# One layer of a hybrid attention, convolution and MoE block: q/k stacks two tiles late, rotation ahead of the head norm, expert weights by half rows

## The chip, the cores and the metric

One Trainium2 chip, of which the program uses one core. The time of a run is the device time of that core in microseconds (us). The core has five engines that each work through an instruction list of their own, in order: TensorE (PE, matmuls and transposes; PEld is its weight load), VectorE (DVE), ScalarE (ACT), GpSimd (POOL) and SyncE (SP, which mostly issues DMAs). The order within each list is fixed when the program is built. PSUM is the memory that PE writes to, SBUF the memory of the other operands.

## The reference

```python
def in_proj(h, w_in, q_g, k_g):
    z = h @ w_in
    ...
    q = rms_norm(q.reshape(b, s, N_HEADS, HEAD_DIM), q_g)
    k = rms_norm(k.reshape(b, s, N_KV_HEADS, HEAD_DIM), k_g)
...
def apply_axial_rope(x, cos, sin):
    xs = x.reshape(*x.shape[:-1], 2, 2, ROPE_FREQS)
    x1, x2 = xs[..., 0, :], xs[..., 1, :]
    c, s = cos[:, None], sin[:, None]
    return jnp.stack([x1 * c - x2 * s, x1 * s + x2 * c], axis=-2).reshape(x.shape)
...
    hx = rms_norm(x, norm1_g) * (1.0 + sc1) + sh1
    hc = rms_norm(ctx, norm1_g) * (1.0 + csc1) + csh1
    qx, kx, vx, bx, cx, ux = in_proj(hx, w_in, q_norm_g, k_norm_g)
    qc, kc, vc, bc, cc, uc = in_proj(hc, w_in, q_norm_g, k_norm_g)
    qx = apply_axial_rope(qx, cos, sin)
    kx = apply_axial_rope(kx, cos, sin)
...
    ax = latent_attention(qx, k_all, v_all)
    convx = short_conv(bx, cx, ux, conv_w)
    x_new = x + gt1 * merge_out(ax, convx, attn_out_g, conv_out_g, w_out)
    hx2 = rms_norm(x_new, norm2_g) * (1.0 + sc2) + sh2
    x_new = x_new + gt2 * hier_moe(hx2, w_group, w_router, w_gate, w_up, w_down)
...
    def expert_block(args):
        xb, e = args
        return (jax.nn.silu(xb @ w_gate[e]) * (xb @ w_up[e])) @ w_down[e]
```

There are 2048 latent tokens and 256 context tokens of 1024 features, 8 query heads and 2 key/value heads of 64, 8 channel groups of the convolution, and 32 experts of width 768 with two experts for each token. Everything is float32 in the inputs and the output. The output is the final RMSNorm of x_new.

## The kernel before

Matmuls run in float16 on split operands: a float32 value is written as a high part (a cast) and a low part (the value minus the high part), and three matmuls (high by high, high by low, low by high) stand for one.

**Projection of q, k and v** (45 to 285 us). The tokens go by chunks of 256 (two tiles of 128): one of context, then eight of latent tokens. `norm_load` brings two tiles `xt` in and scales their rows (L184 on ACT, L186 on POOL). `norm_T` works for the next chunk: for each of 8 feature blocks k, PE transposes (L268), ACT applies the modulation into `hf` (L270), DVE makes the high part of `h` (L271) and the low part (L272), each 128x256. `project` computes for a tile 24 pairs of matmuls into `pq` (L303, 512 columns) and `pk` (L304, 256 columns), and after each block k calls the generator `beside`, which lets other work into PE's list between the matmuls. `head_norm` follows: squares on ACT (L314, L315), their sum `ssq` (L318, DVE), the reciprocal root `qnr` by a power on POOL (L117), the product with q and k out of PSUM into `z` (L321, L322), the rotation by `rope` out of SBUF (L288, L292, L293), the float16 stacks `ks` and `qs` (ACT L333, L339; DVE L334, L340). The rotation tables, norm gain included, are made for all ten heads on POOL (L283). `stacks` transposes `ks` and `qs` on PE (L347, L348, L357) and ACT copies them out (L349, L350, L358). Its steps are written into the last two blocks of the next tile's projection and the first two of the tile after that; the scheduler may place PE's instructions somewhat off those places. In PE's list the `ks` transposes of a chunk's first tile stand in the last block (k = 7) of the next tile's projection, those of its second tile in the second block (k = 1) of the tile after next.

**Attention, convolution, output projection and routing** (285 to 1565 us) aren't written differently by the change. `mod2` computes the second half of the modulation row by row on DVE there (`macc`, L655), from DMAs on SP.

**Experts** (1565 to 2624 us). `PLAN` is a fixed list that mixes large and small experts (room for 104 to 208 tokens). `Stream` brings each expert's weights in as six pieces of 1536 KB (`raw`, 5 buffers, DMAs on SP) and splits each in three steps (L1192 on ACT, L1194 on DVE, 128x1024 each) into `wr` (6 buffers). `gate_up` goes over 6 column blocks f: 24 matmuls for gate, 24 for up (L1338 to L1340), then silu (ACT L1356), product (DVE L1357), cast (ACT L1358) and low part (DVE L1359) into `a`; after each of the first five f come three split steps. `down` (more than 128 tokens, with `rows_out`, L1412 and L1413) or `down_rows` (L1396, L1399) holds four. Pieces are column halves: gate 1, up 1, gate 2, up 2, down 1, down 2, so that a row of a DMA is 384 or 512 numbers long. `transposes` (L1332 to L1334) makes the next expert's input. Results are added to `acc` in DRAM by POOL's indirect DMAs; at the end the final norm loads `acc` through the same `raw` buffers (`final_item`).

Of the kernel before, what the change touches and what calls it, by code (L numbers as in the profile page):

```python
# [19 lines left out]
P = 128  # L20
D = 1024
# [23 lines left out]
WS = 256.0  # L45
NRAW, NRDY, NEARLY = 5, 6, 4
# [12 lines left out]
def tile_block(ctx: ExitStack, tc: tile.TileContext, x, c, ctxt, c_ctx, w_mod, b_mod, norm1_g, w_in,  # L59
# [80 lines left out]
    with ExitStack() as st:  # L140
# [112 lines left out]
        g10 = wp.tile([P, 2, 10, HD], F32, name="g10")  # L253
        V.tensor_copy(g10[:, 0, 0:8], gqk[:, 0:1].to_broadcast([P, 8, HD]))
        V.tensor_copy(g10[:, 0, 8:10], gqk[:, 1:2].to_broadcast([P, 2, HD]))
        gs = [g10[:, i].rearrange("p h (a b f) -> p (h a) b f", a=2, b=2) for i in range(2)]
# [5 lines left out]
        def norm_T(xs, ch):  # L262
            i = 1 if ch < 0 else 0
            h = hcur[ch] = hp.tile([P, 2, KT, CH], F16, name="h")
            for k in range(KT):
                tp = pp.tile([P, CH], F32, name="tp", bufs=2)
                for j, xn in enumerate(xs):
                    T.transpose(tp[:, j * P:(j + 1) * P], xn[:, k * P:(k + 1) * P], ident)  # L268
                hf = sp.tile([P, CH], F32, name="hf")
                A.activation(hf, tp, AF.Identity, scale=AB[:, i, 0, k:k + 1], bias=AB[:, i, 1, k:k + 1])  # L270
                V.tensor_copy(h[:, 0, k, :], hf)  # L271
                V.tensor_sub(h[:, 1, k, :], hf, h[:, 0, k, :])  # L272
                if k == KT - 1 and ch >= 0:
                    nc.scalar.dma_start(hs[ch], h.rearrange("p a k t -> p (a k t)"))
                yield

        def rope_tables(tt):
            rt_ = qp.tile([P, 2, HD], F32, name="rt_")
            nc.sync.dma_start(rt_[:, 0], rope_c[tt * P:(tt + 1) * P, :])
            nc.sync.dma_start(rt_[:, 1], rope_s[tt * P:(tt + 1) * P, :])  # L280
            tab = qp.tile([P, 2, 10, HD], F32, name="tab")
            for i in range(2):
                G.tensor_tensor(tab[:, i], g10[:, i], rt_[:, i:i + 1].to_broadcast([P, 10, HD]), op=OP.mult)  # L283
            return tab

        def rope(dst, z, tab):
            t1 = qp.tile([P, 10, HD], F32, name="rp1", bufs=1)
            V.tensor_mul(t1, z, tab[:, 0])  # L288
            t2 = qp.tile([P, 10, HD], F32, name="rp2", bufs=1)
            zv, tv, sv = [t.rearrange("p h (a b f) -> p (h a) b f", a=2, b=2) for t in (z, t2, tab[:, 1])]  # L290
            for b in range(2):
                V.tensor_mul(tv[:, :, b], zv[:, :, 1 - b], sv[:, :, b])  # L292
            V.tensor_add(dst, t1, t2)  # L293
# [14 lines left out]
        def head_norm(pq, pk, tt, lat, tab):  # L308
            kt = tt + 2 if lat else tt
            nh = 10 if lat else 2  # L310
            z = qp.tile([P, 10, HD], F32, name="z")
# [4 lines left out]
            A.activation(vf[:, kt, :], pk[:, 128:256], AF.Copy, scale=1.0 / WS)  # L316
            ssq = qp.tile([P, 10], F32, name="ssq")
            V.tensor_reduce(ssq[:, 0:nh], sq[:, 0:nh], axis=AX.X, op=OP.add)  # L318
            r = rstd_of(qp, ssq[:, 0:nh], nh, 1.0 / (HD * WS * WS), "qn")
            if lat:  # L320
                V.tensor_mul(z[:, 0:8], pq.rearrange("p (h d) -> p h d", d=HD), r[:, 0:8, None].to_broadcast([P, 8, HD]))  # L321
            V.tensor_mul(z[:, nh - 2:nh], pk[:, 0:128].rearrange("p (h d) -> p h d", d=HD),  # L322
                         r[:, nh - 2:nh, None].to_broadcast([P, 2, HD]))
            V.tensor_reduce(vmx[:, kt:kt + 1], vf[:, kt, :], axis=AX.X, op=OP.max, apply_absolute_value=True)
            if lat:
                zr = qp.tile([P, 10, HD], F32, name="zr")
                rope(zr, z, tab)
            else:
                V.tensor_mul(z[:, 0:2], z[:, 0:2], gqk[:, 1:2].to_broadcast([P, 2, HD]))
                zr = z  # L330
# [41 lines left out]
        for ch in range(-1, NCH):  # L372
# [3 lines left out]
            for j in range(CH // P):  # L376
# [3 lines left out]
                def beside(first, second, j=j):  # L380
# [9 lines left out]
                z = project(h, j, lat, beside(done, nxt))  # L390
# [3 lines left out]
                if len(done) > 1:  # L394
                    for _ in done.pop(0):
                        pass
# [3 lines left out]
            if ch + 2 < NCH:  # L400
                xs = norm_load(ch + 2, (A, G))
# [729 lines left out]
    HE = DE // 2  # L1131
    PW = KT * HE

    def piece_src(e, i):
        if i < 4:
            src = (w_gate, w_up)[i % 2][0, bass.ds(e, 1)].rearrange("a (k p) n -> p (a k) n", p=P)
            return src[:, :, (i // 2) * HE:(i // 2 + 1) * HE], KT
        src = w_down[0, bass.ds(e, 1)].rearrange("a (k p) n -> p (a k) n", p=P)
        return src[:, :, (i - 4) * 512:(i - 3) * 512], FT

    class Stream:
# [62 lines left out]
        def get(self, q):  # L1204
            while self.piece <= q:
                assert self.step()
            return self.ready[q].rearrange("p a (k n) -> p a k n", k=KT if q % 6 < 4 else FT)
# [92 lines left out]
    with ExitStack() as st:  # L1300
# [16 lines left out]
        def gather(il):  # L1317
            xg = []
            for i, (t, o, n) in enumerate(il):
                g_ = xp.tile([P, D], F32, name=f"xg{i}", bufs=3 - i)  # L1320
# [15 lines left out]

        def three(p_, w, k, cs, x, C, first, last):
            T.matmul(p_[:, :C], w[:, 0, k, cs], x[:, 0, k, :C], start=first, stop=False)  # L1338
            T.matmul(p_[:, :C], w[:, 0, k, cs], x[:, 1, k, :C], start=False, stop=False)  # L1339
            T.matmul(p_[:, :C], w[:, 1, k, cs], x[:, 0, k, :C], start=False, stop=last)  # L1340
# [266 lines left out]
```

## Time and profile before

| | us |
|---|---|
| median of 3 runs | 2630.31 (2628.85 to 2637.18) |
| profiled execution | 2625.82 |
| its span | 2624.0 |
| PE busy | 2333.0 (89%) |
| DVE busy | 2064.2 (79%) |
| ACT busy | 1678.6 (64%) |
| POOL busy | 726.3 (28%) |
| mean granted clock of PE | 0.95 of full speed |

The span is the time from the first to the last instruction that the profile holds; the 1.8 us that the execution takes beyond it lie around it. An engine is busy while it works on an instruction; matmuls overlap in PE's pipeline, so that the durations of single matmuls add up to more than PE's busy time. A wait is put down to the instruction that ended it. The granted clock says how fast PE was allowed to run: 1.0 is 2.4 GHz and 0.5 is 1.2 GHz, and means lie between. The chain of waits is followed back from the last instruction, at each step to what released it.

### The profile page before, as it was taken

How to read it: one execution, taken by the hardware profiler on the slowest of the kernel's cores; microseconds unless marked ns; L12 is line 12 of the kernel's file. 1: busy time of each engine (PE TensorE's matmuls, PEld its weight loads, DVE VectorE, ACT ScalarE, POOL GpSimd, SP SyncE). 2: the span in 40 equal slices, each digit the busy share in tenths (PEclk: the TensorE clock that was granted, in tenths of full speed). 3: DMA queues.
4: the chain of work that ended last, by engine and by line, in shares of the span. 5: the costliest groups of instructions: out<-in, count | busy, mean ns of one | idle time of the engine just before them, and what ended most of it. 6: DMA issues, size and time to landing. Idle time of an engine off the chain costs nothing. (4 is left out here: it accounts for less than half of the span.)

```text
span 2624.0 us, 65043 instructions
## 1 busy us (share of the span) xinstructions
PE 2333.0 (89%) x26923; PEld 1791.5 (68%) x26923; DVE 2064.2 (79%) x3558; ACT 1678.6 (64%) x3170; POOL 726.3 (28%) x449
## 2 busy tenths in 40 slices
PE   7878898898999999888889949999999999999974
PEld 2545565665777755555555539998899988999953
DVE  4786789999777788878897657788788887788866
ACT  4554365566666676556656427777677777888854
POOL 2554114322222234435444331111111111211122
PEclk9888999999999999889998969999999999999987
DMA  7422423323111143212211569999999999999996
GB/s 279 145 90 88 127 78 115 125 82 108 50 52 34 34 93 81 64 52 80 58 64 52 191 197 336 338 326 304 307 355 350 349 334 344 340 335 340 358 311 247
DMA packets 320331, 499.27 MB, mean 190 GB/s; under 512 B 50466, under 2 KB 229022, under 8 KB 316959
## 3 DMA queue, kind: packets, MB, share of 16 engines
q1 hardware_dynamic: 281142, 429.41, 48.7%
q0 software_dynamic: 16032, 39.85, 6.0%
q10 hardware_dynamic: 22856, 25.82, 2.9%
q8 instruction: 212, 3.47, 0.5%
q14 instruction: 89, 0.72, 0.1%
HBM read 427.20 MB, written 67.90 MB: 189 GB/s over the span
## 5 line engine op out<-in xcount | busy, mean ns | idle before, releaser
L1194 DVE SCALAR_TENSOR_TENSOR wr<-raw,wr 128x1024 f16<-128x1024 f32 x576 | 685.4, 1218 | 118.8 <-ACT wr L1192 111.3
L1192 ACT ACTIVATE wr<-raw 128x1024 f16<-128x1024 f32 x576 | 580.4, 1054 | 57.3 <-DMA raw<-in_w_up_dram 22.9
L489 ACT ACTIVATE pf<-st 128x512 f32<-128x512 f32 x576 | 345.0, 599 | 284.2 <-PE st L488 226.9
L496 POOL TENSOR_TENSOR pl<-pf,ph 128x1024 f16<-128x1024 f32 x125 | 273.5, 2188 | 620.0 <-PE o L514 259.3
L461 DVE TENSOR_REDUCE mx<-mxp 128x1 f32<-128x512 f32 (+1 forms) x640 | 391.9, 628 | 65.1 <-PE mxp L460 63.6
L1339 PEld LDWEIGHTS <-wr 128*128 128x128 f16 x4032 | 397.4, 99 | 27.6 <-issue 24.6
L1340 PEld LDWEIGHTS <-wr 128*128 128x128 f16 x4032 | 397.2, 99 | 14.4 <-issue 9.9
L1338 PEld LDWEIGHTS <-wr 128*128 128x128 f16 x4032 | 397.1, 99 | 14.1 <-issue 11.3
L490 ACT ACTIVATE ph<-st 128x512 f16<-128x512 f32 x576 | 344.6, 598 | 0.0
L1338 PE MATMUL pg<-x,wr 128*128 128x152 f16 (+19 forms) x1536 | 293.9, 226 | 6.7 <-ACT sg L1356 3.8
L1338 PE MATMUL pu<-x,wr 128*128 128x152 f16 (+19 forms) x1536 | 293.7, 226 | 5.2 <-DVE sg L1357 5.1
L1340 PE MATMUL pu<-x,wr 128*128 128x152 f16 (+19 forms) x1536 | 293.1, 226 | 1.6 <-DVE wr L1194 0.8
L1340 PE MATMUL pg<-x,wr 128*128 128x152 f16 (+19 forms) x1536 | 293.5, 226 | 1.1 <-DVE wr L1194 1.0
L1339 PE MATMUL pg<-x,wr 128*128 128x152 f16 (+19 forms) x1536 | 293.8, 226 | 0.0
L1339 PE MATMUL pu<-x,wr 128*128 128x152 f16 (+19 forms) x1536 | 293.5, 226 | 0.0
L613 PE MATMUL z<-h,cwh 128*128 128x256 f16 x1536 | 275.1, 275 | 12.9 <-DVE vb L621 8.9
L460 PE MATMUL mxp<-k1T,q 128*128 128x512 f16 (+1 forms) x640 | 230.9, 364 | 41.5 <-DVE mx L461 40.5
L514 PE MATMUL o<-vh,pl 128*128 128x65 f16 x2304 | 246.2, 196 | 7.0 <-DVE pl L498 4.6
L512 PE MATMUL o<-vh,ph 128*128 128x65 f16 x2304 | 247.0, 197 | 0.3 <-ACT ob L521 0.2
L513 PE MATMUL o<-vlo,ph 128*128 128x64 f16 x2304 | 246.8, 195 | 0.0
L512 PEld LDWEIGHTS <-ph 128*128 128x128 f16 x2304 | 217.6, 99 | 25.2 <-issue 9.8
L487 PE MATMUL st<-q,k1T 128*128 128x512 f16 x576 | 222.5, 387 | 12.4 <-ACT ph L490 11.9
(349 smaller groups left out, 5541.6 us busy)
## 6 DMA issues: line engine op xcount, KB each, us to landing
raw<-in_w_down_dram SPq DMA_DIRECT2D x64, 1536.0 KB
raw<-in_w_gate_dram SPq DMA_DIRECT2D x63, 1536.0 KB
raw<-in_w_up_dram SPq DMA_DIRECT2D x63, 1536.0 KB
xt<-in_x_dram SPq DMA_DIRECT2D x32, 512.0 KB
h<-hs SPq DMA_DIRECT2D x16, 1024.0 KB
wmod<-in_w_mod_dram SPq DMA_DIRECT2D x64, 256.0 KB
w<-in_w_mod_dram SPq DMA_DIRECT2D x16, 512.0 KB
hs<-h ACTq DMA_DIRECT2D x8, 1024.0 KB
```

What stands on the lines that cost most here:

```text
L461: V.tensor_reduce(rowmax[u][:, j, i:i + 1], p_[:, :n], axis=AX.X, op=OP.max)
L489: A.activation(pf[:, i], p_, AF.Exp)
L490: A.activation(ph[:, i], p_, AF.Exp)
L496: G.tensor_tensor(pl, pf, ph, op=OP.subtract)
L512: T.matmul(po[:, j], ph[:, i, js], vh1[:, k, g], start=f, stop=False, skip_group_check=True)
L513: T.matmul(po[:, j, 0:HD], ph[:, i, js], vlo[:, k, g], start=False, stop=False, skip_group_check=True)
L613: T.matmul(z, w_[:, k, cs], h[:, a_, k, :], start=(n == 0), stop=(n == 3 * KT - 1))
L1192: A.activation(w[:, 0, sl], t[:, sl], AF.Copy, scale=WS)
L1194: V.scalar_tensor_tensor(w[:, 1, sl], t[:, sl], WS, w[:, 0, sl], op0=OP.mult, op1=OP.subtract)
L1338: T.matmul(p_[:, :C], w[:, 0, k, cs], x[:, 0, k, :C], start=first, stop=False)
L1339: T.matmul(p_[:, :C], w[:, 0, k, cs], x[:, 1, k, :C], start=False, stop=False)
L1340: T.matmul(p_[:, :C], w[:, 1, k, cs], x[:, 0, k, :C], start=False, stop=last)
```

## The change

It has five parts.

1. `beside` steps one generator, the stacks of the tile two back, at the odd blocks k of the projection.
2. `head_norm` rotates q and k straight out of PSUM (`pq`, `pk`), adds, and only then multiplies by the head norm (one product over all ten heads, L334 of the change). The tables `tab` hold one row for q and one for k.
3. `norm_T` makes the high and the low part of `h` for four feature blocks at once (`HB`, 128x1024), and moves on at the even blocks k, and at all blocks of a chunk's second tile.
4. The second `xt` of a chunk is scaled on ACT.
5. Expert pieces are halves by rows (gate 1, gate 2, up 1, up 2, down 1, down 2), so that a DMA's row is 768 or 1024 numbers long. `gate_up` does the six gate blocks, then the six up blocks, with one split step after each; `down` and `down_rows` use both halves from their start and hold six steps.

```diff
+HB = 4
...
-        g10 = wp.tile([P, 2, 10, HD], F32, name="g10")
...
+        gx = wp.tile([P, 2, HD], F32, name="gx")
...
         def norm_T(xs, ch):
...
+            for b in range(KT // HB):
+                hf = sp.tile([P, HB, CH], F32, name="hf")
+                for k2 in range(HB // 2):
+                    tp = pp.tile([P, 2, CH], F32, name="tp", bufs=2)
...
+                    if k2 == HB // 2 - 1:
+                        ks = slice(b * HB, (b + 1) * HB)
+                        V.tensor_copy(h[:, 0, ks], hf)
+                        V.tensor_sub(h[:, 1, ks], hf, h[:, 0, ks])
...
-                G.tensor_tensor(tab[:, i], g10[:, i], rt_[:, i:i + 1].to_broadcast([P, 10, HD]), op=OP.mult)
+            for i, g_ in enumerate((gqk, gx)):
+                G.tensor_tensor(tab[:, i], g_, rt_[:, i:i + 1].to_broadcast([P, 2, HD]), op=OP.mult)
...
+        def rope(zr, pq, pk, tab):
...
+            for o, n, src, i in ((0, 8, pq, 0), (8, 2, pk[:, 0:2 * HD], 1)):
+                zv = src.rearrange("p (h d) -> p h d", d=HD)
+                V.tensor_tensor(t1[:, o:o + n], zv, tab[:, 0, i:i + 1].to_broadcast([P, n, HD]), op=OP.mult)
...
+                for b in range(2):
+                    V.tensor_tensor(ts[:, :, :, b], zs[:, :, :, 1 - b], ss_[:, :, :, b].to_broadcast([P, n, 2, 16]), op=OP.mult)
+            V.tensor_add(zr, t1, t2)
...
-                V.tensor_mul(z[:, 0:8], pq.rearrange("p (h d) -> p h d", d=HD), r[:, 0:8, None].to_broadcast([P, 8, HD]))
...
+            V.tensor_mul(zr[:, 0:nh], zr[:, 0:nh], r[:, 0:nh, None].to_broadcast([P, nh, HD]))
...
+                def beside(behind, second, j=j):
                     for k in range(KT):
-                        if k < 2 and len(first) > 1:
-                            next(first[0], None)
-                        if k >= KT - 2 and first:
-                            next(first[-1], None)
-                        if k % 2 or (j and k == KT - 2):
+                        if k % 2 and behind:
+                            next(behind, None)
+                        if k % 2 == 0 or j:
                             next(second, None)
                         yield
...
+                behind = done.pop(0) if len(done) > 1 else None
+                z = project(h, j, lat, beside(behind, nxt))
...
-                xs = norm_load(ch + 2, (A, G))
+                xs = norm_load(ch + 2, (A, A))
...
+    KN = (KT // 2, KT // 2, FT // 2)
+    PW = KT // 2 * DE
...
+        kn = KN[i // 2]
+        src = (w_gate, w_up, w_down)[i // 2][0, bass.ds(e, 1)].rearrange("a (k p) n -> p (a k) n", p=P)
+        return src[:, (i % 2) * kn:(i % 2 + 1) * kn, :], kn
...
+        def both(self, q):
+            return self.get(q), self.get(q + 1)
...
+            sg = sp.tile([P, FT, CM], F32, name="sg", bufs=1)
+            for m in range(2):
+                w = ws.both(q0 + 2 * m)
+                for f in range(FT):
+                    p_ = pp.tile([P, 512], F32, name=("pg", "pu")[f % 2])
+                    for k in range(KT):
+                        three(p_, w, k, slice(f * P, (f + 1) * P), x, C, k == 0, k == KT - 1)
+                    next(side, None)
+                    if m == 0:
+                        A.activation(sg[:, f, :C], p_[:, :C], AF.Silu, scale=1.0 / WS)
+                    else:
...
+                    ws.step()
```

PE at the `ks` transposes of the first tile of the fourth latent chunk (tile 6, counted from 0), before:

```order
L304 LDWEIGHTS h
L304 MATMUL pk<-wh,h 128x256
L347 LDWEIGHTS ks
L347 MATMUL tq<-ident_h,ks 128x128
L268 MATMUL tp<-ident,xt 128x128
L348 LDWEIGHTS ks
L348 MATMUL tq<-ident_h,ks 66x128
```

and with the change:

```order
L312 LDWEIGHTS h
L312 MATMUL pq<-wh,h 128x512
L313 LDWEIGHTS h
L313 MATMUL pk<-wh,h 128x256
L351 LDWEIGHTS ks
L351 MATMUL tq<-ident_h,ks 128x128
L352 LDWEIGHTS ks
L352 MATMUL tq<-ident_h,ks 66x128
```

Before, these rows stand in the last block of tile 7's projection, after 21 of its 24 matmuls into `pq`; with the change in the third block of tile 8's, after 6 of 24. So a chunk's first tile has its `ks` transposed nine pairs of matmuls later, and a second tile three to four pairs later (after 6 of 24 in place of 2 or 3).

DVE from the norm to the rotation of one tile, before (`rp_1560` and `rp_1562` are the two products of the rotation):

```order
L115 TENSOR_SCALAR qnv<-ssq 128x10
L324 TENSOR_REDUCE vmx<-vf 128x1
L321 TENSOR_TENSOR z<-pq,qnr 128x512
L322 TENSOR_TENSOR z<-pk,qnr 128x128
L288 TENSOR_TENSOR rp_1560<-z,tab 128x640
L292 TENSOR_TENSOR rp_1562<-z,tab 128x20x16 x2
L271 CAST h<-hf 128x256
L293 TENSOR_TENSOR zr<-rp_1560,rp_1562 128x640
L272 TENSOR_TENSOR h<-hf,h 128x256
L271 CAST h<-hf 128x256
```

and with the change:

```order
L298 TENSOR_TENSOR rp_1703<-pq,tab 128x512
L301 TENSOR_TENSOR rp_1704<-pq,tab 128x16x16 x2
L298 TENSOR_TENSOR rp_1703<-pk,tab 128x128
L301 TENSOR_TENSOR rp_1704<-pk,tab 128x4x16 x2
L331 TENSOR_REDUCE ssq<-sq 128x10
L302 TENSOR_TENSOR zr<-rp_1703,rp_1704 128x640
L116 TENSOR_SCALAR qnv<-ssq 128x10
L333 TENSOR_REDUCE vmx<-vf 128x1
L277 CAST h<-hf 128x1024
L334 TENSOR_TENSOR zr<-zr,qnr 128x640
L278 TENSOR_TENSOR h<-hf,h 128x1024
```

The rotation stands ahead of the sum of squares, the norm's product `zr<-zr,qnr` comes last, and one wide cast and one wide difference of `h` stand where narrow ones were. The power on POOL lies between `qnv` and that product.

ACT where an expert for 124 tokens is followed by one for 176, before:

```order
L1192 ACTIVATE wr<-raw 128x1024 x3
L1358 CAST a<-sg 128x124
L1192 ACTIVATE wr<-raw 128x1024 x6
L1356 ACTIVATE sg<-pg 128x176
L1192 ACTIVATE wr<-raw 128x1024
L1333 CAST x<-tq 128x4x120
L1192 ACTIVATE wr<-raw 128x1024 x2
L1333 CAST x<-tq 128x4x120
```

and with the change:

```order
L1362 CAST a<-sg 128x124
L1192 ACTIVATE wr<-raw 128x1024 x10
L1336 CAST x<-tq 128x4x120
L1359 ACTIVATE sg<-pg 128x176
L1359 ACTIVATE sg<-pu 128x176
L1336 CAST x<-tq 128x4x120
L1359 ACTIVATE sg<-pg 128x176
```

Ten split steps instead of six stand in a row there, and the silus `sg` of the next expert come behind them without splits between.

Two things move that the diff doesn't write: some twenty DMAs of `mod2` and of the output projection's weights stand earlier on SP, in the projection stage, and eight `macc` instructions of DVE (L655) stand in its first three tiles instead of at the start of the attention.

## Rows read from the trace of the kernel before

**Rows 1.** Stretches: start:end, length, busy of PE, PEld, DVE, ACT, POOL, clock, DMA, GB/s.
```profile
58.00:273.00 215.00, 171.17 (x1079) 105.48 (x1077) 162.44 (x347) 110.79 (x247) 109.43 (x66) 0.89 0.34 108
273.00:285.00 12.00, 3.03 (x19) 2.08 (x18) 7.70 (x21) 6.42 (x16) 1.95 (x1) 0.71 0.44 122
...
1600.00:2000.00 400.00, 389.72 (x5018) 365.50 (x5016) 320.49 (x421) 296.70 (x490) 68.25 (x38) 1.00 1.01 328
2000.00:2480.00 480.00, 458.75 (x6708) 439.58 (x6706) 389.20 (x523) 379.40 (x662) 79.12 (x55) 0.99 1.03 344
2480.00:2585.00 105.00, 77.32 (x1090) 64.07 (x1088) 77.57 (x112) 69.95 (x125) 20.30 (x21) 0.90 0.93 330
```

**Rows 2.** Waits of PE, 57 to 273 us: us in total, times, longest.
```profile
PE tq L348 <- DVE ks L334: 23.0, 14, 3.2
PE tq L347 <- ACT ks L333: 18.0, 8, 4.0
```

**Rows 3.** Timeline, 180 to 200 us: start, length, engine, line, instruction, [idle before].
```profile
190.58 2.17 DVE L293 TENSOR_TENSOR zr<-rp,rp 128x640 f32<-128x640 f32 x1
...
193.24 0.29 PE L347 MATMUL tq<-ident_h,ks 128*128 128x128 f16 x1 [4.04 <-ACT ks L333]
```

**Rows 4.** Instructions of L303: durations min/median/max ns, first and last start.
```profile
L303 PE MATMUL pq<-wh,h x256: 379/379/634, 57.9 to 272.2; 128*128 128x512 f16 x128
```

**Rows 5.** Waits of DVE, 57 to 273 us.
```profile
DVE z L321 <- POOL qnr L117: 21.0, 11, 2.1
DVE h L271 <- ACT hf L270: 15.3, 13, 3.7
DVE ssq L318 <- ACT sq L315: 10.8, 10, 2.2
```

**Rows 6.** DMA queue q1 in 30 to 45 us, then 1600 to 2000: packets, MB, share.
```profile
q1 hardware_dynamic: 2423, 5.85, 100.0%
...
q1 hardware_dynamic: 72108, 114.95, 83.9%
```

**Rows 7.** Waits of all engines, 1600 to 2500 us.
```profile
ACT a L1358 <- DVE sg L1357: 120.0, 69, 3.3
...
PE pg L1338 <- ACT a L1358: 19.0, 18, 3.5
```

**Rows 8.** Chain of waits near the end: start us, length, what.
```profile
2505.58 8.27 DMA raw<-acc
...
2550.44 12.85 DMA raw<-in_w_gate_dram
...
2568.68 11.74 DMA raw<-acc
```

**Rows 9.** Instructions of L271, L272, L764 and L498: durations min/median/max ns.
```profile
L271 DVE CAST h<-hf x72: 277/286/2015, 45.4 to 251.2; 128x256 f16<-128x256 f32 x72
...
L272 DVE TENSOR_TENSOR h<-hf,h x72: 408/424/1770, 45.7 to 251.6; 128x256 f16<-128x256 f32 x72
...
L764 DVE CAST mh<-mf x24: 343/410/2352, 947.3 to 1412.7; 128x384 f16<-128x384 f32 x12, 128x512 f16<-128x512 f32 x12
...
L498 DVE TENSOR_TENSOR pl<-pf,ph x163: 1201/1218/3360, 330.1 to 1454.9; 128x1024 f16<-128x1024 f32 x163
```

**Rows 10.** Groups of instructions by form, 45 to 285 us: busy us, mean ns, idle before.
```profile
L117 POOL TENSOR_TENSOR qnr<-qnv,mhalf 128x10 f32<-128x10 f32 x16 | 32.2, 2013 | 55.6 <-DVE qnv L115 46.8 <-DVE vm L408 8.0 <-DVE n1v L115 0.7
...
L293 DVE TENSOR_TENSOR zr<-rp,rp 128x640 f32<-128x640 f32 x16 | 17.1, 1071 | 0.1
...
L288 DVE TENSOR_TENSOR rp<-z,tab 128x640 f32<-128x640 f32 x16 | 14.5, 905 | 0.2
L292 DVE TENSOR_TENSOR rp<-z,tab 128x320 f32<-128x320 f32 x32 | 14.1, 482 | 0.0
```

**Rows 11.** Instructions of L655: durations min/median/max ns.
```profile
L655 DVE SCALAR_TENSOR_TENSOR macc<-wmod,scT,macc x56: 729/742/2639, 292.8 to 647.2; 128x512 f32<-128x512 f32 x56
```

**Rows 12.** Groups by form, 1600 to 2500 us: the same columns.
```profile
L1192 ACT ACTIVATE wr<-raw 128x1024 f16<-128x1024 f32 x512 | 516.6, 1055 | 50.5 <-DMA raw<-in_w_up_dram 19.5 <-DMA raw<-in_w_down_dram 16.5 <-PE pg L1396 7.4
```

More of the change, by code (lines that the diff above doesn't have):

```diff
@@ L310, in head_norm @@
             nh = 10 if lat else 2
-            z = qp.tile([P, 10, HD], F32, name="z")
+            zr = qp.tile([P, 10, HD], F32, name="zr")
             sq = qp.tile([P, 10, HD], F32, name="sq", bufs=1)
@@ L393, in tile_block @@
                         next(cws, None)
-                if len(done) > 1:
-                    for _ in done.pop(0):
-                        pass
+                for _ in behind or ():
+                    pass
                 done.append(stacks(*head_norm(*z, tt, lat, tab), tt, lat))
@@ L1337, in three @@
         def three(p_, w, k, cs, x, C, first, last):
-            T.matmul(p_[:, :C], w[:, 0, k, cs], x[:, 0, k, :C], start=first, stop=False)
-            T.matmul(p_[:, :C], w[:, 0, k, cs], x[:, 1, k, :C], start=False, stop=False)
-            T.matmul(p_[:, :C], w[:, 1, k, cs], x[:, 0, k, :C], start=False, stop=last)
+            n = w[0].shape[2]
+            w_, kk = w[k // n], k % n
+            T.matmul(p_[:, :C], w_[:, 0, kk, cs], x[:, 0, k, :C], start=first, stop=False)
+            T.matmul(p_[:, :C], w_[:, 0, kk, cs], x[:, 1, k, :C], start=False, stop=False)
@@ L1342, in gate_up @@
+            T.matmul(p_[:, :C], w_[:, 1, kk, cs], x[:, 0, k, :C], start=False, stop=last)
         def gate_up(x, ws, q0, C, side=iter(())):
             a = xp.tile([P, 2, FT, CM], F16, name="a")
-            for hf in range(2):
-                gw, uw = ws.get(q0 + 2 * hf), ws.get(q0 + 2 * hf + 1)
-                for f3 in range(3):
-                    f = hf * 3 + f3
-                    ps = []
-                    for w, tag in ((gw, "pg"), (uw, "pu")):
-                        p_ = pp.tile([P, 512], F32, name=tag)
-                        for k in range(KT):
-                            three(p_, w, k, slice(f3 * P, (f3 + 1) * P), x, C, k == 0, k == KT - 1)
-                        ps.append(p_)
-                        next(side, None)
-                    sg = sp.tile([P, CM], F32, name="sg")
-                    A.activation(sg[:, :C], ps[0][:, :C], AF.Silu, scale=1.0 / WS)
-                    V.scalar_tensor_tensor(sg[:, :C], ps[1][:, :C], 1.0 / WS, sg[:, :C], op0=OP.mult, op1=OP.mult)
-                    A.copy(a[:, 0, f, :C], sg[:, :C])
-                    V.tensor_sub(a[:, 1, f, :C], sg[:, :C], a[:, 0, f, :C])
-                    for _ in range(3 if f < FT - 1 else 0):
-                        ws.step()
-                ws.done(q0 + 2 * hf)
-                ws.done(q0 + 2 * hf + 1)
@@ L1389, in down_rows @@
             y = sp.tile([P, D], F32, name="y", bufs=3)
-            ws_ = [ws.get(q0 + 4 + b) for b in range(2)]
+            w = ws.both(q0 + 4)
             py = [pp.tile([P, 512], F32, name=tag) for tag in ("pg", "pu")]
@@ L1400, in down_rows @@
                                        gt2r[:n, b * 512:(b + 1) * 512], op0=OP.mult, op1=OP.mult)
-                ws.step()
-                ws.step()
+                for _ in range(3):
+                    ws.step()
                 ws.done(q0 + 4 + b)
```

90 lines of the change are left out of this document (36 added, 54 removed).

## The prediction

> **What bounds the kernel now.** I read the busy time by stretches first [rows 1]. The expert stretches are nearly full: PE works 389.72 of 400 us and 458.75 of 480, so that 10.3 and 21.3 us, some 32 together, are all that better order could give back there. The projection stage is not full: from 58 to 273 us PE works 171.17 of 215 us, DVE 162.44, and the mean granted clock is only 0.89. No engine is the bound; they wait for one another. So the next view is the waits. PE loses 23.0 + 18.0 = 41 us there to transposes of the key stack `ks` [rows 2]. The timeline shows one such place [rows 3]: the rotation's sum L293 takes 2.17 us from 190.58, the cast to `ks` can start only then, and PE has stood idle for 4.04 us when its transpose begins at 193.24. The matmuls into `pq` that follow such pauses run up to 634 ns where the least is 379 [rows 4]; the long ones stand at the lower of the two granted levels, 1.2 in place of 2.4 GHz, so a pause costs more than its length. DVE on its side waits 21.0 us for the power on POOL, 15.3 us for `hf` and 10.8 us for the squares [rows 5]; the last two come from ACT, which waits for PE's transposes and matmuls. This is a ring: PE waits for DVE's late `ks`, and DVE for work that the stalled PE delivers late.
>
> Among the experts the DMA engines are full (share 1.01 and 1.03 [rows 1]). Between 1600 and 2000 us the weights' queue q1 holds 83.9% of 16 engines' time for 114.95 MB [rows 6], and PE's largest wait is 19.0 us for the cast of `a`, behind ACT's 120.0 us for DVE's product `sg` [rows 7]: engines whose queues are filled with splits of pieces that land late. At the end the last transfers stand in the chain themselves, 8.27, 12.85 and 11.74 us long [rows 8].
>
> **The projection stage.** Its 16 latent tiles start their first matmul at 57.9 us and their last at 272.2 [rows 4]: 214.3/16 = 13.4 us a tile. What could a tile take?
>
> PE: 171.17 us at a mean clock of 0.89 [rows 1] are 152 us at full clock, 9.5 a tile. ACT: 110.79/16 = 6.9, and the second `xt` of a chunk, moved from POOL, adds under 1. Neither binds.
>
> DVE works 162.44/16 = 10.15 us a tile [rows 1]. *Removed:* for each chunk eight casts and eight differences of 256 columns, 8 x (0.286 + 0.424) = 5.7 us by the medians [rows 9]. *Added:* two casts and two differences of 1024 columns. A cast takes 0.34 for 384 and 0.41 for 512 columns, which carries on to 0.68 for 1024; a difference of 1024 columns took 1.22 [rows 9]: 2 x 1.90 = 3.8 us. So 1.9 us less a chunk, 0.95 a tile. *Moved:* norm and rotation pass 640 columns four times, before as after; I take them as equal, with 0.15 more for the two additional instructions (between ends of -0.3, as the full-width products L288 and the sum L293, 0.905 and 1.071 at the mean [rows 10], may get quicker beside a less busy POOL, and +0.5, as out of PSUM the halves may take more than L292's 0.482). That gives 10.15 - 0.95 + 0.15 = 9.35 us of work.
>
> *Waits:* the power takes 2.0 us [rows 10]. The rotation now stands ahead of it, but DVE issues the sum, then `qnv`, and has only the maximum of `v`, and in half of the tiles a wide cast, before the product that needs the power. So I leave the wait as it is, 21.0/16 = 1.3 us a tile [rows 5]. What goes is the ring. The first tile of a chunk has its `ks` transposed nine pairs of matmuls later, 9/24 of 9.5 = 3.6 us, and the longest waits are 3.2 and 4.0 us [rows 2]; a second tile gains only three to four pairs, some 1.4 us, but waits less now. Of the 26.1 us for `hf` and the squares [rows 5], 1.6 a tile, I keep 0.3. Sum: 9.35 + 1.3 + 0.3 = 11.0 us a tile, and 16 x (13.4 - 11.0) = **-38 us**. Ends: 10.1 a tile if the work sheds its contention (-53), 12.6 if the ring stays (-13).
>
> Around it: the first `h` comes later, once, as its half needs four `hf` and 1.9 us of DVE in place of 0.71 (**+2**, ends 0 and +4). Behind the last tile 12 us pass to 285 [rows 1], in which the rotation no longer follows the power (**-2**, ends 0 and -4). Eight `macc` instructions of 0.742 us [rows 11] leave the start of the attention, 5.9 us of DVE, of which I take half as on the path, **-3** (ends 0 and -6). In the first three tiles, where they go, DVE's waits cover them.
>
> **The experts.** PE's matmuls and the split steps keep their number. What changes is the transfer: rows of 768 and 1024 numbers in place of 384 and 512. The only price in the trace for longer packets is the stretch from 30 to 45 us, where q1 holds the engines whole: 240 us of engine time for 5.85 MB in 2423 packets, 24.4 bytes a ns at 2.4 KB a packet. From 1600 to 2000 us it is 0.839 x 6400 = 5370 us for 114.95 MB in 72108 packets, 21.4 bytes a ns at 1.6 KB [rows 6]. At the better rate 192 pieces, 302 MB, need 108 us less of all 16 engines, and the share falls from 1.02 to some 0.92. Pieces land sooner, splits run earlier, and part of PE's 32 idle us goes. Against that stand later uses: both halves of `down` are needed at its start. I take **-18**, a little over half (ends -32 and +5), **-2** for the first experts' pieces, and **-5** near the end, where some 28 us of PE are idle [rows 1] and the transfers of [rows 8] get shorter (ends -17 and +7).
>
> **Sum:** -38 + 2 - 2 - 3 - 18 - 2 - 5 = -66 us. The profiled execution took 2625.8 us, which gives 2559.8; the runs' median lies 4.5 above it: **2564 us**. About 0.3%, 8 us, is what a measurement of this kernel tells from no change.
>
> **Rivals.** *The ring stays* (0.14). DVE gets `h` in halves of 1024 columns, so that a product that PE waits for can stand 1.9 us behind a cast and a difference; and for second tiles "two tiles late" was true before to within four pairs. Then a tile takes 12.6 us, 26 us more in all: 2590. For it speaks that DVE is busy only 76% of the stretch [rows 1] while others wait for it; against it that the places of the longest waits get 3.6 us. The Trainium skill, Perfetto Trace Analysis, section Optimizing Scalar/DVE Operations, says as much: where these engines aren't saturated but cause bubbles elsewhere, breaking instructions up may let work complete sooner, while grouping helps a saturated engine. By its first half the sum would be this rival's, by the rows above it is the forecast's.
>
> *Bytes cost what they cost* (0.12). The better rate from 30 to 45 us may belong to a stretch in which no other queue runs, and not to longer packets. Then the share stays at 1.0, and the last three terms go from -25 to -2: 2587. The Trainium skill, DMA: Bandwidth & Descriptors, section Why small descriptors are slow, points this way: about 3 cycles for a packet beside one for 32 bytes, which by my estimate saves 3% on rows twice as long, where the rows above give 12%. Both rivals together (0.06): 2613.
>
> *All of it* (0.10): a tile falls to PE's 9.5 us (-24 more), the experts' idle time goes whole (-14) and half of the end's (-8): 2518.
>
> *Slower: ACT's list among the experts* (0.08). Where a large expert follows a small one ten splits of 1.055 us [rows 12] stand ahead of its silus in place of six, 4.2 us more, at nine places of the plan: 38 us. If PE also waits for `a` at the turn of each expert as long as it now does 18 times, 19.0/18 = 1.06 us [rows 7], that is 34 us more. With 72 in place of -20: 2564 + 92 = 2656. It decides from 46/32 = 1.4 us an expert, where the other terms are eaten up. Against it: two pairs of PSUM buffers let PE run four blocks ahead, and 24 matmuls at 389.72/5018 us each are 1.9 us.
>
> **How the numbers follow.** The forecast has 0.50, with its own range of 2543 to 2586. The range from 2528 to 2612 leaves out the slower case and most of the best. Faster by over 0.3% are all cases but the last and the worst edge of the third: 0.87; the same 0.05, slower 0.08.
>
> **What would show it.** Right: waits of PE for `ks` under 15 us in the stage, `pq` at 379 ns nearly throughout and a clock near 0.97, tiles at 10.7 to 11.3 us, DVE busy near 0.87; packets of 3 and 4 KB on q1 at 24 bytes a ns, a DMA share of 0.92 and PE at 0.98 between 1600 us and 2400. Wrong: DVE's waits for `hf` unchanged or a `ks` wait of over 2 us in each tile (the ring); engine time for a byte as before; PE waiting for silu behind splits at the turns of experts.

## The result and the profile after

The changed kernel takes 2567.38 us (median of 4 runs, 2561.39 to 2569.17) beside 2633.74 us before (4 runs). The ratio is 0.9748, with a 95% interval of 0.9730 to 0.9767. The profiled execution took 2567.82 us, its span is 2566.0 us against 2624.0 before: 58.0 us less, while the medians differ by 66.4 us.

Where the 58 us went is read from the first matmul of each stage in the two traces. The column for the forecast holds the prediction's terms.

| stretch | before | after | difference | forecast |
|---|---|---|---|---|
| first `pq` matmul of a latent tile | 57.9 | 59.4 | +1.5 | +2 |
| 16 latent tiles | 214.3 (13.4 each) | 162.7 (10.2 each) | -51.6 | -38 |
| last `pq` matmul to first scores | 21.2 | 21.3 | +0.1 | -2 |
| first to last scores | 1112.2 | 1118.0 | +5.8 | -3 |
| last scores to first gate matmul | 159.9 | 159.5 | -0.4 | 0 |
| first gate matmul to last down matmul | 1040.6 | 1028.3 | -12.3 | -18 - 2 |
| from there to the end | 17.9 | 16.8 | -1.1 | -5 |

The stretches of the changed kernel (columns as in [rows 1]) answer to those rows.

```profile
59.50:223.00 163.50, 152.84 (x1062) 98.24 (x1063) 118.20 (x273) 107.86 (x241) 51.83 (x57) 0.99 0.45 145
223.00:240.00 17.00, 8.73 (x50) 5.81 (x49) 11.42 (x31) 9.90 (x21) 1.96 (x1) 0.61 0.59 152
...
1555.00:1955.00 400.00, 391.32 (x5050) 366.19 (x5048) 322.67 (x420) 302.07 (x497) 73.39 (x38) 1.00 0.97 333
1955.00:2435.00 480.00, 469.10 (x6919) 449.14 (x6917) 399.48 (x538) 391.18 (x684) 84.33 (x56) 0.99 1.01 353
2435.00:2527.00 92.00, 62.18 (x861) 50.83 (x859) 68.25 (x103) 57.67 (x102) 19.79 (x20) 0.85 0.89 326
```

In the projection stage PE is now 93% busy at a clock of 0.99 where it was 80% at 0.89. DVE's work fell from 162.44 us in 215 to 118.20 in 163.5. Among the experts PE went from 97.4% and 95.6% to 97.8% and 97.7%, and the share of the DMA engines only from 1.01 and 1.03 to 0.97 and 1.01.

PE's waits up to 300 us, against [rows 2]:

```profile
PE tp L271 <- ACT hf L272: 6.3, 8, 1.5
...
PE tp L271 <- ACT xt L185: 4.5, 2, 2.7
PE tq L352 <- DVE ks L338: 1.8, 6, 0.5
```

The waits for the key stack, 41 us before, are 1.8 us. The `pq` matmuls, against [rows 4], still reach 634 ns, but few of them do: their mean is 381 ns, where it was 404.

```profile
L312 PE MATMUL pq<-wh,h x256: 379/379/634, 59.4 to 222.1; 128*128 128x512 f16 x128
```

DVE's waits from 57 to 240 us, against [rows 5]:

```profile
DVE zr L334 <- POOL qnr L118: 30.0, 18, 2.0
...
DVE h L277 <- ACT hf L272: 4.4, 4, 1.5
DVE rp L298 <- ACT sq L323: 4.1, 7, 1.3
```

The power on POOL is waited for as before, and more: 30.0 us in place of 21.0. The waits for `hf` and for the squares fell from 26.1 to 8.5 us.

DVE's groups of instructions, 45 to 240 us (columns as in [rows 10]), hold what the prediction did not see:

```profile
L278 DVE TENSOR_TENSOR h<-hf,h 128x1024 f16<-128x1024 f32 x18 | 22.0, 1222 | 0.3
...
L302 DVE TENSOR_TENSOR zr<-rp,rp 128x640 f32<-128x640 f32 x16 | 16.0, 1001 | 0.0
...
L277 DVE CAST h<-hf 128x1024 f16<-128x1024 f32 x18 | 12.4, 689 | 8.5 <-ACT hf L272 8.2 <-DMA rt__1165<-in_rope_c_dram 0.3
...
L298 DVE TENSOR_TENSOR rp<-pq,tab 128x512 f32<-128x512 f32 x16 | 11.0, 687 | 4.1 <-ACT sq L323 4.1
L344 DVE TENSOR_TENSOR qs<-zr,qs 128x512 f16<-128x512 f32 x16 | 11.0, 686 | 1.1 <-ACT qs L343 1.1
...
L116 DVE TENSOR_SCALAR qnv<-ssq 128x10 f32<-128x10 f32 x16 | 2.6, 160 | 0.0
```

The narrow casts and differences of the kernel before, 45 to 285 us:

```profile
L272 DVE TENSOR_TENSOR h<-hf,h 128x256 f16<-128x256 f32 x72 | 48.6, 676 | 1.0
L271 DVE CAST h<-hf 128x256 f16<-128x256 f32 x72 | 38.2, 532 | 17.9 <-ACT hf L270 17.7
```

Wide casts (0.689) and differences (1.222) cost what was forecast, 0.68 and 1.22. But the narrow ones had means of 0.532 and 0.676 over the medians of 0.286 and 0.424 in [rows 9]: the sum over 72 of each was 86.8 us, where the medians give 51.1. The difference lies in 27 of the 144, which took 1.4 to 2.0 us; each of the 27 ran beside one of POOL's table products (L283) or scalings of `xt` (L186). Now the sum is 34.4.

### The profile page after: what moved, and what is told of

It is laid out like the page before. It is cut to its first block, busy times and chain, and to the rows that moved or that the text cites. A ratio compares the mean times of both kernels' runs of the same rounds, so it can differ in the third digit from the quotient of the medians.

```text
span 2566.0 us, 64760 instructions
## 1 busy us (share of the span) xinstructions
PE 2317.3 (90%) x26923; PEld 1784.0 (70%) x26923; DVE 2013.4 (78%) x3480; ACT 1684.5 (66%) x3177; POOL 673.4 (26%) x442
## 5 line engine op out<-in xcount | busy, mean ns | idle before, releaser
L1192 ACT ACTIVATE wr<-raw 128x1024 f16<-128x1024 f32 x576 | 587.4, 1055 | 79.8 <-DMA raw<-in_w_down_dram 23.8
L498 POOL TENSOR_TENSOR pl<-pf,ph 128x1024 f16<-128x1024 f32 x125 | 273.4, 2187 | 621.8 <-PE o L516 274.3
```

The lines of the kernel that those rows point to most:

```text
L498: G.tensor_tensor(pl, pf, ph, op=OP.subtract)
L1192: A.activation(w[:, 0, sl], t[:, sl], AF.Copy, scale=WS)
```

## The experiments

Times are medians of runs on the same chip with the kernel before; "first scores" and "a tile" are read from each trace as in the table above (before: 293.4 and 13.4 us, changed: 243.4 and 10.2). Kernels with the same projection have their first scores within some 2 us of each other (243.4, 245.3 and 243.5 in the changed kernel, e1 and e3, 293.4 and 295.5 before and in e2), so that smaller differences say nothing.

### The two halves alone (e1, e2)

e1 is the kernel before with all edits outside the experts, e2 the kernel before with those to the experts (`piece_src`, `gate_up`, `down`, `down_rows`, `gather`) alone.

> The projection edits (parts 1 to 4) with the experts of before. Theory A (the two halves of the change don't touch each other; the projection gives 50 us up to the first scores, and some of it is lost by chance of the clock in the attention): first scores near 243 us, a time of 2578 to 2590, ratio 0.980 to 0.984. Rival B (the projection's gain is given back later whenever DMAs of the attention come earlier; the experts pay the rest): first scores near 243 us but a time above 2595.

> The experts by half rows with the projection of before. Theory A: the expert stage, 1040 us before from its first gate matmul to its last down matmul and 1028 with the change, takes 1026 to 1032 us here too, and the time is 2616 to 2624, ratio 0.992 to 0.997. Rival B (the expert stage is quicker only with the other half, as its first pieces come earlier or later): 1034 us or more, ratio above 0.997.

e1: 2580.42 us beside 2629.11, ratio 0.9825 (0.9794 to 0.9855), first scores at 245.3 us, experts 1040.7 us. e2: 2612.29 us, ratio 0.9936 (0.9918 to 0.9955), experts 1024.1 us. The product of the two ratios is 0.9762, beside 0.9748 for the whole: the halves add up. Theory A holds for e1; e2 has its ratio, and gains somewhat more than it said (1026 to 1032 us for the experts, 2616 to 2624 in all). Some 70% of the gain are the projection's.

### Short rows in the new order (e3)

```diff
-    self.queue.dma_start(t.rearrange("p (k n) -> p k n", k=k), src)
+    td = t.rearrange("p (k n) -> p k n", k=k)
+    nh = td.shape[2] // 2
+    for c2 in range(2):
+        self.queue.dma_start(td[:, :, c2 * nh:(c2 + 1) * nh], src[:, :, c2 * nh:(c2 + 1) * nh])
```

> The changed kernel, each expert piece brought in by two DMAs of column halves, so that rows are 384 and 512 numbers long as before, with the new order of the experts kept. Theory A (longer rows give what the experts gained: 22.9 to 23.2 bytes a ns on q1 in place of 21.4 to 21.8): the rate falls back to 21.3 to 21.9 and the time rises by 8 to 20 us to 2575 to 2588. Rival B (the new order of gate and up blocks gave it, and DMA time is covered): the rate falls, the time stays within 4 us of 2567. Rival C (the order alone is worse than before, and longer rows more than pay for it): above 2590.

2579.71 us, ratio 0.9818 (0.9786 to 0.9850). The queue q1 in 880 us among the experts, of the kernel before, the changed one and e3 (packets, MB, share of 16 engines):

```profile
q1 hardware_dynamic: 163202, 261.39, 85.8%
```

```profile
q1 hardware_dynamic: 87294, 267.39, 82.5%
```

```profile
q1 hardware_dynamic: 166668, 262.59, 86.1%
```

Engine time is the share times 14080 us: 12081 us for 261.39 MB are 21.6 bytes a ns before, 23.0 after, 21.7 in e3. So a byte costs 6% less on rows twice as long. The experts take 1035.9 us in e3. In the nine kernels with the changed kernel's experts (it, e2, e4 to e10) they take 1023.3 to 1030.6 us, in the three with those of before (it, e1, e11) 1040.6 to 1040.7. So longer rows are worth 5 to 12 us there, and the time lies in theory A's range. The 5 us that are left to the new order of the blocks are less than the spread of those nine, and aren't shown. Of the 12 us that e3 loses, 5.7 lie ahead of the experts, between the last scores and the first gate matmul (165.2 us in place of 159.5). The kernel before, with rows as short, takes 159.9 there, so that these are not the rows' price; e3 also brings each piece in by two DMAs in place of one.

### The power beside the rotation (e4)

```diff
+            ssq = qp.tile([P, 10], F32, name="ssq")
+            V.tensor_reduce(ssq[:, 0:nh], sq[:, 0:nh], axis=AX.X, op=OP.add)
+            r = rstd_of(qp, ssq[:, 0:nh], nh, 1.0 / (HD * WS * WS), "qn")
             if lat:
                 rope(zr, pq, pk, tab)
...
-            ssq = qp.tile([P, 10], F32, name="ssq")
-            V.tensor_reduce(ssq[:, 0:nh], sq[:, 0:nh], axis=AX.X, op=OP.add)
-            r = rstd_of(qp, ssq[:, 0:nh], nh, 1.0 / (HD * WS * WS), "qn")
```

> The changed kernel with the sum of squares and the power's input ahead of the rotation, so that the power runs beside the rotation. DVE waited 30.0 us for the power in the changed kernel. Theory A (a tile is bound by PE now, 152.84 of 163.5 us busy): DVE's wait falls under 8 us, a tile goes from 10.17 to 9.9 to 10.2 us, and the time falls by 0 to 5 us. Rival B (DVE's chain from the projection to the key stack is the bound): a tile falls to 9.0 to 9.6 us and the time by 9 to 18 us.

2550.68 us (2547.98 to 2554.03), ratio 0.9710 (0.9680 to 0.9739): every run is quicker than the quickest of the changed kernel, 2561.39. DVE's wait for the power fell from 30.0 to 5.2 us. A tile takes 9.8 us, between the two theories and nearer to A's 9.9 to 10.2 than to B's 9.0 to 9.6; the time fell by 16.7 us, which A had at 5 or less. The first scores stand at 233.7 us, 9.7 earlier, of which the tiles give 5.9 and the way from the last tile to the scores 3.2, where the last power now runs beside the last rotation. Neither theory had counted that. The remaining difference of the medians lies in the attention and the experts, which differ by as much between kernels that share their code, and isn't put down to the edit; by the two ratios, each against the kernel before in its own set of runs, the gain is 0.0038, or 10 us, though their intervals overlap. PE's stretch shows that little is left in the tiles, 96% busy:

```profile
58.90:216.00 157.10, 150.86 (x1061) 98.14 (x1062) 120.69 (x275) 108.13 (x241) 65.87 (x57) 0.99 0.48 152
```

### The stacks at their old places (e5)

```diff
-                def beside(behind, second, j=j):
+                def beside(first, second, j=j):
                     for k in range(KT):
-                        if k % 2 and behind:
-                            next(behind, None)
+                        if k < 2 and len(first) > 1:
+                            next(first[0], None)
+                        if k >= KT - 2 and first:
+                            next(first[-1], None)
...
```

> The changed kernel with the stacks' steps at their old places in the projection (last two blocks of the next tile, first two of the one after). Theory A (DVE's work, not the place of the stacks, set the tile: DVE fell from 162 to 118 us busy): PE meets its key stacks in time nearly as well, a tile takes 10.2 to 10.8 us. Rival B (the forecast's ring: the late stacks are what opened it): PE waits for the stacks return with 20 us or more and a tile takes 11.5 us or more.

2577.61 us in one run, a tile 10.9 us, first scores at 254.0 us. PE's waits for the stacks:

```profile
PE tq L351 <- ACT ks L337: 13.5, 9, 6.5
PE tq L352 <- DVE ks L338: 3.5, 5, 0.9
```

17 us of waits come back and the scores come 10.6 us later. Each theory has the wrong size: a tile lies a little above A's span, and far from B's 11.5.

### Norm ahead of the rotation, and narrow splits of h (e6, e7)

```diff
...
+                V.tensor_mul(z[:, 0:8], pq.rearrange("p (h d) -> p h d", d=HD), r[:, 0:8, None].to_broadcast([P, 8, HD]))
+                V.tensor_mul(z[:, 8:10], pk[:, 0:128].rearrange("p (h d) -> p h d", d=HD), r[:, 8:10, None].to_broadcast([P, 2, HD]))
+                rope(zr, z, tab)
...
```

> The changed kernel with the head norm ahead of the rotation again (norm out of PSUM, rotation out of SBUF, small tables kept). Theory A (the order alone matters little, as the power was waited for before and after): a tile takes 10.2 to 10.8 us. Rival B (the rotation beside the power is what shortens the chain to the key stack): 11.2 us or more.

2562.83 us in one run, a tile 10.3 us, first scores at 246.6 us, 3.2 later. Theory A: in the tiles the order of rotation and norm is worth nearly nothing by itself, as the prediction had it. Half of the 3.2 us, hardly more than kernels with the same projection differ by, lies behind the last tile.

```diff
+                        V.tensor_copy(h[:, 0, k], hf[:, 2 * k2 + kk])
+                        V.tensor_sub(h[:, 1, k], hf[:, 2 * k2 + kk], h[:, 0, k])
...
-                        V.tensor_copy(h[:, 0, ks], hf)
-                        V.tensor_sub(h[:, 1, ks], hf, h[:, 0, ks])
```

> The changed kernel with casts and differences of h of 256 columns, 16 a chunk in place of 4, all else kept. Theory A (the narrow ones cost DVE 0.286 + 0.424 us when nothing disturbs them, 0.95 us a tile more than the wide ones, and POOL is quiet now): a tile takes 10.4 to 11.2 us, the mean cast 0.28 to 0.35 us. Rival B (they were slow in themselves, 0.547 us a cast at the mean): the mean cast stays above 0.45 us and a tile takes 11.5 us or more.

2572.92 us in one run, first scores at 249.8 us, 6.4 later (a tile takes 10.9 us, but the first starts 4.6 us earlier). Theory A. The narrow casts and differences of e7:

```profile
L274 DVE TENSOR_TENSOR h<-hf,h 128x256 f16<-128x256 f32 x72 | 30.1, 425 | 0.7
L273 DVE CAST h<-hf 128x256 f16<-128x256 f32 x72 | 20.0, 291 | 12.3 <-ACT hf L272 12.0
```

Their means are now the medians of before, 0.291 and 0.425. They were not slow in themselves.

### POOL's old work back (e8, e9, e10)

e8 makes the tables for ten heads and scales the second `xt` on POOL, e9 only the first, e10 only the second.

```diff
...
-            tab = qp.tile([P, 2, 2, HD], F32, name="tab")
-            for i, g_ in enumerate((gqk, gx)):
-                G.tensor_tensor(tab[:, i], g_, rt_[:, i:i + 1].to_broadcast([P, 2, HD]), op=OP.mult)
+            tab = qp.tile([P, 2, 10, HD], F32, name="tab")
+            for i in range(2):
+                G.tensor_tensor(tab[:, i], g10[:, i], rt_[:, i:i + 1].to_broadcast([P, 10, HD]), op=OP.mult)
...
-                xs = norm_load(ch + 2, (A, A))
+                xs = norm_load(ch + 2, (A, G))
```

> The changed kernel with POOL's old work back: rotation tables for all ten heads (two products of 640 columns in place of 128) and the second xt of each chunk scaled on POOL. Theory A (the small POOL work is what took DVE's contention away: DVE's busy time fell by 44 us where the wider splits account for 15): DVE's busy time from the first to the last projection rises by 15 us or more and a tile takes 11.0 us or more. Rival B (the products out of PSUM and the wide splits don't meet POOL): DVE's busy time rises by less than 6 us and a tile stays under 10.6 us.

> The changed kernel with rotation tables for all ten heads on POOL (128x640 in place of 128x128), the second xt kept on ACT. With both of POOL's old tasks back the first scores came 38.6 us later. Theory A (the table products start when the rotation frees their buffer, so that they meet DVE's sum of the rotation and stand ahead of the power on POOL): most of it comes back, first scores 20 to 35 us later than 243.4. Rival B (the xt scaling, 1.9 us long, is the harm): less than 10 us.

> The changed kernel with only the second xt of each chunk scaled on POOL. Theory A: first scores 4 to 15 us later than 243.4, eight scalings of some 1.9 us, beside which DVE's differences out of SBUF stand still. Rival B: 25 us or more.

One run each: e8 2614.66 us, a tile 12.4 us, first scores at 282.0, 38.6 us later than in the changed kernel; e9 2597.34 us, 11.8 us, 274.2, 30.8 later; e10 2573.23 us, 10.6 us, 250.9, 7.5 later. Theory A in all three. The parts add up, 30.8 + 7.5 = 38.3. The tiles of e8 (columns as in [rows 1]):

```profile
63.50:262.00 198.50, 166.61 (x1060) 101.42 (x1059) 156.36 (x273) 100.22 (x233) 102.37 (x64) 0.94 0.37 120
```

DVE works 156.36 us there for instructions that took 118.20, and that difference, 38 us, is as large as the whole delay. Its groups in e8 show which ones grew, against those of the changed kernel above (L302, L116, L344 and L298 there):

```profile
L304 DVE TENSOR_TENSOR zr<-rp,rp 128x640 f32<-128x640 f32 x16 | 25.0, 1561 | 0.0
...
L116 DVE TENSOR_SCALAR qnv<-ssq 128x10 f32<-128x10 f32 x16 | 21.4, 1339 | 0.0
L346 DVE TENSOR_TENSOR qs<-zr,qs 128x512 f16<-128x512 f32 x16 | 18.7, 1169 | 1.8 <-ACT qs L345 1.8
...
L300 DVE TENSOR_TENSOR rp<-pq,tab 128x512 f32<-128x512 f32 x16 | 11.0, 687 | 7.0 <-ACT sq L325 7.0
```

The sum of the rotation went from 1.001 to 1.561, the tiny `qnv` from 0.160 to 1.339, the low part of `qs` from 0.686 to 1.169. The products out of PSUM, which read the larger tables, kept their time (0.687 for the largest), so that the tables' size does no harm on DVE; no table product of POOL runs beside them. The timeline of e8 shows how:

```profile
185.57 0.81 DVE L333 TENSOR_REDUCE ssq<-sq 128x10 f32<-128x640 f32 x1
...
185.73 3.62 POOL L291 TENSOR_TENSOR tab<-g,rt__1881 128x640 f32<-128x640 f32 x2 [4.21 <-DVE rp L303]
...
186.30 1.65 DVE L304 TENSOR_TENSOR zr<-rp,rp 128x640 f32<-128x640 f32 x1
...
187.87 1.50 DVE L116 TENSOR_SCALAR qnv<-ssq 128x10 f32<-128x10 f32 x1
...
189.46 1.96 POOL L118 TENSOR_TENSOR qnr<-qnv,mhalf 128x10 f32<-128x10 f32 x1
...
257.55 0.81 DVE L304 TENSOR_TENSOR zr<-rp,rp 128x640 f32<-128x640 f32 x1
...
258.28 0.17 DVE L116 TENSOR_SCALAR qnv<-ssq 128x10 f32<-128x10 f32 x1
```

POOL's two table products start at 185.73, the moment the rotation's last product has freed their buffer, and so always beside the same DVE instructions: the sum of squares keeps its 0.81, the rotation's sum takes 1.65 and `qnv` 1.50. So it is in 14 of the 16 tiles; in the last two, of which the first stands at 257.55, no table product runs beside them, and the same instructions take 0.81 and 0.17. The power, which the head norm waits for, also stands behind the tables in POOL's list, but it can't start before `qnv` ends at 189.37, and DVE's wait for it, 30.0 us in the changed kernel, did not grow:

```profile
DVE zr L336 <- POOL qnr L118: 29.8, 18, 1.9
```

So the delay is DVE's longer work, and not the place of the power behind the tables. In e10, where only `xt` is on POOL, the rotation's sum is quick and the low part of `qs` pays:

```profile
L344 DVE TENSOR_TENSOR qs<-zr,qs 128x512 f16<-128x512 f32 x16 | 18.7, 1168 | 1.6 <-ACT qs L343 1.6
...
L302 DVE TENSOR_TENSOR zr<-rp,rp 128x640 f32<-128x640 f32 x16 | 15.5, 969 | 0.0
```

### A quiet POOL in the kernel before (e11)

The same two edits, the other way round, on the kernel before, and nothing else; the rotation's products come for q and k apart, as its tables do.

> The kernel before with two edits alone: rotation tables per head kind (POOL 128x128 in place of 128x640) and the second xt scaled on ACT. Stacks, order of norm and rotation, narrow splits of h and the experts are those of before. Theory A (POOL's work, not the ring of late stacks, is what held the projection stage): first scores 20 us or more earlier than 293.4, a time of 2590 to 2612, ratio 0.985 to 0.993. Rival B (the ring holds; quiet POOL helps only with the other edits): less than 10 us earlier, ratio above 0.996.

2600.53 us beside 2627.92, ratio 0.9898 (0.9879 to 0.9917), first scores at 267.8 us, 25.6 earlier. Theory A. The tiles of e11, and PE's wait for the stacks there:

```profile
55.00:245.00 190.00, 160.93 (x1065) 95.98 (x1062) 128.41 (x385) 113.34 (x247) 74.78 (x59) 0.98 0.43 136
```

```profile
PE tq L347 <- ACT ks L333: 20.9, 13, 5.6
```

DVE works 128.41 us, 34 less than before, the clock is 0.98, and this with the stacks at their old places and still 20.9 us of waits for them. Half of the 50 us that the projection gained come with these few lines.

### The final norm's loads later (e12)

```diff
-FIN, AHEAD = (3, 5, 7, 13, 14, 15), 4
+FIN, AHEAD = (5, 7, 9, 13, 14, 15), 4
```

> The kernel of e4 (power beside the rotation) with the first three loads of the final norm two expert pieces later (FIN 5, 7, 9 in place of 3, 5, 7). In e4 ACT's first square of the final norm waits 11.35 us for its load of acc, with splits queued behind it. Theory A (that wait holds the splits of the last experts on the path to the end): ACT's wait falls under 4 us and the time by 4 to 10 us from 2550.7. Rival B (the last pieces then come later, or the tail has other work to cover): within 3 us of 2550.7, or slower.

2551.43 us (2544.96 to 2554.65), ratio 0.9709 (0.9679 to 0.9740): the same as e4. ACT's waits near the end, in e4 and in e12:

```profile
ACT sq L1466 <- DMA raw<-acc: 11.3, 1, 11.3
```

```profile
ACT sg L1359 <- PE pg L1346: 9.5, 1, 9.5
...
ACT sq L1466 <- DMA raw<-acc: 3.5, 1, 3.5
```

The wait of 11.3 us for the load fell to 3.5, but ACT then waited 9.5 us for a gate block of PE, and the time is rival B's: the wait moved.

## Why the prediction was right, point by point

**In sum**, 2564 us was forecast and 2567.38 measured, inside the forecast's own range of 2543 to 2586; the medians differ by 66.4 us where 66 were forecast. That it comes so close is in part luck. In the profiled executions, which differ by 58.0 us, the tiles gave 13.6 us more than forecast, and less came from the attention (8.8), the experts (7.7), the end (3.9) and the way behind the last tile (2.1). Of the signs of being right, the `ks` waits (1.8 us), the clock (0.99) and PE's 0.98 among the experts came; a tile (10.2 us, not 10.7 to 11.3), DVE's share (118.20 of 163.5 us, 0.72 and not 0.87), the bytes a ns (23.0 and not 24) and the DMA share (0.99 and not 0.92) did not.

**The tile's sum** gave 9.35 + 1.3 + 0.3 = 11.0 us; 10.2 were measured. Its first term was mis-sized: DVE's work is 118.20/16 = 7.4 us a tile, 2.0 less than forecast, while DVE's waits for the power and for `hf` and the squares were 1.9 + 0.5 in place of 1.3 + 0.3. The step that failed in it is "*Removed*", priced "by the medians": the casts and differences of `h` take 29.9 us in the changed kernel's stretch and took 77.1 in that of [rows 1], so that 47.2/16 = 2.9 us a tile went and not 0.95. "*Moved*" was right: the passes of norm and rotation took 58.4 us (L288, L292, L293, L321, L322) and take 58.9 (L298, L301, L302, L334). The medians hold only where POOL is quiet, as e7 shows; quiet POOL was in the sum only as an end of -0.3 for other products, which "may get quicker beside a less busy POOL". With POOL's old work back the wide splits hardly suffer, but the instructions behind the rotation do, (156.36 - 118.20)/16 = 2.4 us a tile (e8). The row for it was there: the 2.17 us of L293 in [rows 3] are not a late start but this collision, as two table products run beside it:

```profile
190.53 3.61 POOL L283 TENSOR_TENSOR tab<-g,rt__2039 128x640 f32<-128x640 f32 x2 [1.56 <-DVE rp L292]
```

And the maxima of 2015 and 1770 ns in [rows 9] stood beside medians of 286 and 424. I took the medians as the price of what was removed, and the 36 us of instructions above them for chance. The Trainium skill, SBUF — State Buffer, section Who interferes with whom, has the rule: a DVE instruction with two SBUF inputs contends with a GpSimd instruction that reads SBUF, one in a two-port mode contends with GpSimd, and one with at most one SBUF input outside those modes does not. The rows of e8 agree: the rotation's sum, two inputs out of SBUF, takes 1.65 us beside a table product and 0.81 without one, and the sum of squares, with one, keeps its 0.81, though it starts first.

**The wide splits** were priced right one by one. With POOL quiet the single instructions of e7 and of the changed kernel differ by (30.1 + 20.0 - 34.4)/18 = 0.87 us a tile, near the 0.95 of the sum. Instructions that follow one another overlap a little, so that DVE's busy time differs by less, 126 - 118 us or 0.5 a tile, and the first scores by 6.4 us.

**The power** was left as it was, 1.3 us a tile; it is 30.0/16 = 1.9. In DVE's list the rotation stands ahead of the power's input and not beside the power, as the prediction read there; e4 does put it beside, and gets 9.7 us.

**The ring** was the forecast's main story for the waits. Late stacks are worth 10.6 us (e5), where the rival of a ring that stays had 26, and e11 gains 25.6 us with the ring in place. The rival "the ring stays" fell all the same: PE's waits for `ks` are 1.8 us, where under 15 was named.

**Around the tiles**, +2 came as +1.5, and the -2 behind the last tile did not come (21.2 and 21.3 us); the last power is still waited for. With the old order and a quiet POOL, e6 and e11 take 22.9 and 23.3 us there; why the kernel before doesn't stays open. The `macc` instructions (-3) gave nothing: the values' matmuls of the attention, taken in their order, run 48 to 50 us ahead of the kernel before up to 889 us, which is the lead they start with. By 936 us 4 us of it are lost. The attention between the first and last scores, before, after and in e8 (columns as in [rows 1]):

```profile
293.40:1405.60 1112.20, 1025.04 (x11460) 688.22 (x11459) 930.04 (x1707) 690.83 (x1413) 363.72 (x199) 0.97 0.25 74
```

```profile
243.40:1361.40 1118.00, 1028.28 (x11464) 690.85 (x11463) 927.85 (x1701) 691.00 (x1413) 362.81 (x199) 0.96 0.24 72
```

```profile
282.00:1405.80 1123.80, 1031.94 (x11465) 692.45 (x11463) 932.95 (x1702) 690.65 (x1413) 360.88 (x199) 0.96 0.24 71
```

It has nearly the same instructions in all, DVE's work differs by less than 1%, and it takes 1111.1 to 1123.8 us over the kernels here. What decides in a single execution was not tried and stays open.

**The experts** were forecast at -20 and gave -12.3 (-10 to -17 over the kernels with this code), and the end -5 against -1.1. The step that failed is "At the better rate": 24.4 bytes a ns, from a stretch where q1 is alone, against 23.0 measured. Packets of 3 KB and 4 KB cost 6% less a byte and not 12%; the share stayed at 0.99 over the two long stretches and not 0.92. The Trainium skill, DMA: Bandwidth & Descriptors, section Why small descriptors are slow, gives about 3% by my estimate, and the measurement lies between. So the rival "bytes cost what they cost" was half right: it named -2 for what came as -13.4, against -25.

**The slower case** did not come. PE's waits for ACT's `a` and `sg`, 1555 to 2455 us, are less than the 19.0 us of [rows 7], although ten splits stand in a row there:

```profile
PE pg L1344 <- ACT a L1362: 4.1, 12, 0.5
...
PE pg L1344 <- ACT sg L1359: 2.7, 1, 2.7
```

## What to carry to other kernels

Where DVE's instructions of one line have maxima and means far above their median, look at what GpSimd does at those moments before pricing them: work that is "hidden on POOL" was paid on DVE here, 2.4 us a tile, as it started whenever DVE freed a buffer. Count what a change takes off POOL at the price of the DVE instructions beside it, and look in an engine's list for what stands ahead of the one result that others wait for. A rate measured where a queue has the engines to itself is an end of the range, not the likeliest value.

## What the runs showed of the hardware that was not expected

A tensor-scalar instruction of DVE on 128x10 numbers takes 0.160 us in the changed kernel and 1.339 at the mean in e8, beside POOL products of 128x640; a reduction of 128x640 beside the same product keeps its 0.81. The small `qnv` lost more there than the rotation's sum ahead of it, 1.18 us against 0.56. And the granted clock over the tiles was higher where PE idled less: 0.89 with 20% idle before, 0.94 with 16% in e8, 0.98 with 15% in e11 and 0.99 with 7% in the changed kernel.
